# One layer of a hybrid mixer and a mixture of experts on one core: a routing step, prefetch gating and small PE products reordered

## The chip, the cores and the metric

The kernel runs on one core of one Trainium2 chip. The metric is the device time of one execution in microseconds (us). Times are medians of several runs; beside them stands one profiled execution, from which all rows below are taken. Engines are named as the profile names them: PE is TensorE, DVE is VectorE, ACT is ScalarE, POOL is GpSimd, and SP is the engine whose queue issues most of the DMAs. PEld is the loading of PE's stationary operand.

## What is computed

One layer on 1024 tokens of width 1024. A token mixer (a state-space group, a forgetting-attention group and a convolution group behind one input projection and before one output projection) is added to the input; then each token goes to one of four expert groups and, inside it, to two of eight experts. All is float32.

```python
x = x + g_m * hybrid_mixer(rms_norm(x) * (1 + sc_m) + sh_m)
h = rms_norm(x, norm_ffn_g) * (1.0 + sc_f) + sh_f
p_g = softmax(h @ w_rg + b_rg)                # 4 groups, the best one is taken
g_sel = argmax(p_g)
e_logits = (h @ w_re + b_re) of that group    # 8 experts in it
top_p, top_i = top_k(softmax(e_logits), 2)
weights = top_p / sum(top_p) * p_g[g_sel]
# for each of the 32 experts e, on the tokens that chose it:
hid = silu(xb @ w_gate[e]) * (xb @ w_up[e])   # 1024 x 512 each
y  += weight * (hid @ w_down[e])              # 512 x 1024
out = rms_norm(x + g_f * y, final_norm_g)
```

## The kernel before

**Tiling.** The 1024 tokens are eight blocks of 128 rows (`NB`), held with tokens on partitions or, transposed, with features on partitions. Every float32 product on PE is made of three: each operand is split into a rounded part and a rest (`h_hi` and `h_lo`, `xh` and `xl`, `phi` and `plo`), and hi*hi, hi*lo and lo*hi are accumulated in one bank.

**Stages.** First come the products with the conditioning vector (`ada`): chunks `at` of a weight matrix arrive by DMA, and 8 products (L415) make one piece of a row, which two products at L423 (`ps_arr`) then add up. They are spread over the input projection. `qk_tile(t)` for t = 0 to 3 (L182 to L184, `ps_pr`) makes a feature-major tile of the queries and keys, 48 products of 128x512. Between them stands the transpose of `ncu`, the negative running sum of the forget gates, into bank `ps_nc` (L487), copied to `nct` and written to HBM, from where the attention reads it back much later.

**End of the mixer.** For each row block `b` the generator `post_steps` makes the output projection (L994 to L996, `ps_wo`), adds it to the input in two halves of 512 columns (`xb`, L1000), transposes the result (`xT`), takes the root mean square, and makes the router's logits `L`: 8 products with the transposed rows as the moving operand (L1019, `ps_rt`), a copy `rT`, a transpose (L1023), and two additions into `L` (L1024, L1025). The normalized rows `h2` go to `h_d` in HBM (L1034), one DMA of 128x1024 for a block. `route_steps(b0, b1)` takes `L` of some blocks to one-hot choices `oh` and to places in the expert's list: `ps_pos` counts the tokens before a row, `ph` is the one-hot place, `Ev` the one-hot expert times the token number, and `ps_tab` = ph' x Ev is a table of token numbers by place (rows) and expert (columns). The names in the rows carry an r in front (`rohr`, `rph`, `rEv`). After the last block the table becomes the integer `toki` by four operations of DVE (L1135 to L1139): add to `tab`, find the empty places, shift by one, cast. A second use of `ph` (L1167) makes the table of weights `wtab`.

**Experts.** For expert `e` a gather by POOL (L1308, an indirect DMA with `toki`) reads its up to 128 rows of `h_d` into `xg` or `xq`; eight transposes (L1318, bank `ps_xg`) and a split give `xh`, `xl`. The weights come as 192 halves of 1 MB (two for each gate, up and down matrix) into a ring of 18 half-buffers (`NHALF`) named w, wx, wy, xq, cy; wy holds one half in two pieces. SP issues them (L1198), at most three in flight. ACT casts each half to `phi`, DVE subtracts to `plo` (L1328), and PE multiplies: 12 products of 128x512 for a half (L1340 to L1342, `ps_gu`; L1368 to L1370, `ps_d`). The same 25 products of `ident` with itself that the change uses (`WARM`, bank `ps_warm`, L292) stand at the very start of the program.

**What sets the order.** A scheduler orders the instructions of each engine from the data they need; `keep_in_program_order` (`pin` in the diff) holds an instruction at its place among the others so marked, and `tc.issue_after(ins)` or the argument of `load_half` makes an operation wait for `ins`. `NC_` + `POST` = 18 is the ring: `NC_` halves are issued before the first gather, `POST` after it. Before the change the last three of the ring wait behind three tiny memsets of POOL that follow the first gather (L1385). `row_load` and `row_spread` (L1282, `ps_row`) bring a 1024-long row of conditioning (`gf`, used at the end) to all partitions: 8 products from `sl` and two copies by ACT.

Of the kernel before, what the change touches and what calls it, by code (L numbers as in the profile page):

```python
# [12 lines left out]
F32 = mybir.dt.float32  # L13
# [9 lines left out]
P = 128  # L23
T = 1024
D = 1024
NB = 8
# [14 lines left out]
DL = 3  # L41
POST = 3
CP = 11
AN = 4
QD = 1
DC, NC_ = 2, 15
KORD = (4, 5, 6, 7, 0, 1, 2, 3)
# [27 lines left out]
def mixer_moe(ctx, tc, x, pch, prow, ada_m, ada_r, w_col, w_z, w_v, w_dtf, w_out, w_rt, w_gu, w_dn, out):  # L75
# [407 lines left out]
    for t in range(4):  # L483
        qk_tile(t)
        if t == 0:
            pc = bank("ps_nc")
            PE.transpose(pc[:32, 0:P], ncu.rearrange("p h b -> p (h b)"), ident)  # L487
            nct = sa.tile([32, P], F32, name="nct", bufs=1)
            V.tensor_copy(nct, pc[:32, 0:P])
            nc.sync.dma_start(ncum_d.rearrange("h (b k) -> (h b) k", k=P), nct)  # L490
        ada_row(*pend)
        if t == 3:
            v_split(1)
        pend = ada_acc(4 + t)
        drain(6)
# [424 lines left out]
    rank = rtp.tile([P, NB, 3], F32, name="rank")  # L920
    G.iota(vtok, pattern=[[P, NB]], base=1, channel_multiplier=1, allow_small_or_imprecise_dtypes=True)
    xsp = ctx.enter_context(tc.tile_pool(name="xsp", bufs=1, reuse_waits="tile"))
    xqs_both = xsp.tile([P, 2 * D], F32, name="xq1")
# [58 lines left out]
    def c_steps(b, yh, yl, xbs):  # L982
# [5 lines left out]
        for q in range(2):  # L988
            qs_ = slice(512 * q, 512 * (q + 1))
            ps = bank("ps_wo", "pj")  # L990
            for n, kt in enumerate(KORD):
# [7 lines left out]
                yield  # L999
            V.tensor_tensor(xb[:, qs_], ps, xb[:, qs_], op=ALU.add)  # L1000
            S.activation(ps, xb[:, qs_], AF.Square, accum_out=s2[:, q:q + 1])
# [6 lines left out]
    def post_steps(b, xb, xT, s2, h2):  # L1008
# [4 lines left out]
        if b == NB - 1:  # L1013
            tc.keep_in_program_order(V.tensor_tensor(h2, xb, ccn["af"], op=ALU.mult))
        yield
# [10 lines left out]
        yield  # L1026
        if b < NB - 1:
            V.scalar_tensor_tensor(h2, xb, s2[:, 3:4], ccn["af"], op0=ALU.mult, op1=ALU.mult)
            for q in range(2):
                hs = slice(512 * q, 512 * (q + 1))  # L1030
                (V if q else G).tensor_tensor(h2[:, hs], h2[:, hs], ccn["shf"][:, hs], op=ALU.add)
        else:
            V.scalar_tensor_tensor(h2, h2, s2[:, 3:4], ccn["shf"], op0=ALU.mult, op1=ALU.add)
        S.dma_start(h2_d[bs, :], h2)  # L1034
# [16 lines left out]
    tab = sc2.tile([P, NE], F32, name="tab", bufs=1)  # L1051
    tf = sc2.tile([P, NE], F32, name="tf", bufs=1)

    tk = []


    def route_steps(b0, b1):
# [45 lines left out]
        ohr = t_("ohr", NE, dt=F32R)  # L1103
        V.tensor_tensor(ohr, oh[0], oh[1], op=ALU.add)

# [8 lines left out]
        yield  # L1114
        phs, Evs = [], []
        for k in range(2):
            tmp = t_("el4", NE)
            V.tensor_tensor(tmp, ppv, oh[k], op=ALU.mult)
            V.tensor_reduce(pos[:, k, bl], tmp, axis=AX.X, op=ALU.add)
            ph_ = t_(f"ph{k}", P, dt=F32R)  # L1120
            V.tensor_tensor(ph_, i128[:, None, :].to_broadcast([P, n, P]), over(pos[:, k, bl], P), op=ALU.is_equal)
            Ev = t_(f"Ev{k}", NE, dt=F32R)
            V.tensor_tensor(Ev, oh[k], over(vtok[:, bl], NE), op=ALU.mult)
            phs.append(ph_)
            Evs.append(Ev)
            if not lastb:
                yield
        pq_ = bank("ps_tab")
# [3 lines left out]
        if b0 == 0:  # L1132
            V.tensor_copy(tab, pq_[:, 0:NE])
        else:
            V.tensor_tensor(tab, tab, pq_[:, 0:NE], op=ALU.add)  # L1135
        if lastb:
            V.tensor_scalar(tf, tab, 0.0, 8192.0, op0=ALU.is_equal, op1=ALU.mult)
            V.scalar_tensor_tensor(tf, tab, -1.0, tf, op0=ALU.add, op1=ALU.add)
            tk.append(V.tensor_copy(toki, tf).ins)  # L1139
        yield  # L1140
# [117 lines left out]
    run_all(post)  # L1258
    V.tensor_copy(tok_l, tf[:, NE - 1:NE])
    pc_ = bank("ps_cnt")  # L1260
# [24 lines left out]
    row_load(g_rows[0, 3072:4096], sl[0:8, :])  # L1285
    row_spread(gf, sl[0:8, :])

# [18 lines left out]
    with tc.tile_pool(name="ex", bufs=2, reuse_waits="tile") as ex:  # L1306
# [5 lines left out]
        def xpose(e):  # L1312
            xh = ex.tile([P, KT, P], F32R, tag="xh", name="xh", bufs=1)
            xl = ex.tile([P, KT, P], F32R, tag="xl", name="xl", bufs=1)
            for q in range(2):
                pt = bank("ps_xg")
                for j in range(4):
                    PE.transpose(pt[:, j * P:(j + 1) * P], xgs[e % 2][:, (4 * q + j) * P:(4 * q + j + 1) * P], ident)  # L1318
                split(xh[:, 4 * q:4 * q + 4], xl[:, 4 * q:4 * q + 4], pt.rearrange("p (j c) -> p j c", c=P))
            return xh, xl  # L1320
# [61 lines left out]
        g1 = gather(0)  # L1382
        with tc.issue_after(g1.ins):
            for h in halves[NHALF - POST:]:
                G.memset(h[0][:, 0:1], 0.0)  # L1385
        gather(1)
        for _ in range(POST):
            load_half()

# [21 lines left out]
        for e in range(NE):  # L1411
# [227 lines left out]
```

## Time and profile before

| what | value |
|---|---|
| median of 3 runs | 1276.93 us (1276.75 to 1277.41) |
| the profiled execution | 1275.77 us, of which the span from first to last instruction is 1273.9 us |
| mean granted clock of TensorE | 0.972 of full speed |
| PE busy | 1186.6 us, 93% of the span |
| DVE, ACT, POOL busy | 980.5, 736.4, 268.2 us |
| DMA | 313.21 MB, mean 246 GB/s over the span |

The page divides the span into 40 slices of 31.8 us. PE is at nine tenths or more in the slices from 650 us on, where the experts run, and the DMA engines are nearly full there; up to 620 us the mixer runs, with PE at seven to nine tenths or more. Between the two lies the routing of the last block, in which PE has little to do. All times of rows below are microseconds from the start of the span.

### The profile page before, as it was taken

The numbers are of one execution on the slowest core, as the hardware profiler recorded it, in microseconds if no ns is written. First come the engines' busy times: TensorE is split into PE (matmuls) and PEld (weight loads), VectorE is DVE, ScalarE is ACT, GpSimd is POOL, SyncE is SP. The second block draws the span as 40 slices with busy tenths as digits, with TensorE's granted clock in tenths as the row PEclk, the third lists the DMA queues.
The fourth block names the chain that finished last, engine by engine and source line by source line (L and its number), as shares of the span: only waits on it lengthen the run. The fifth ranks groups of instructions, "written<-read, shape, count | busy, mean of one in ns | idle before, by whom it ended". The sixth has DMA issues, their size and how long they took to land. (4 is left out here: it accounts for less than half of the span.)

```text
span 1273.9 us, 17238 instructions
## 1 busy us (share of the span) xinstructions
PE 1186.6 (93%) x6079; PEld 928.3 (73%) x6079; DVE 980.5 (77%) x1395; ACT 736.4 (58%) x1145; POOL 268.2 (21%) x200
## 2 busy tenths in 40 slices
PE   6999989999999779999779999999999999999993
PEld 4676757868678568778568877777877787787772
DVE  4789992145265676575559999999999999999985
ACT  4323322343354656563258877777877787777763
POOL 3110313100100353432111221122112212211112
PEclk9999999999999989999879999999999999999997
DMA  9316667633201553734889999999999999999726
GB/s 361 140 42 220 210 196 224 160 108 89 78 17 59 148 155 100 262 98 183 304 305 343 361 356 372 366 354 367 369 359 372 356 358 387 363 381 366 236 53 257
DMA packets 93339, 313.21 MB, mean 246 GB/s; under 512 B 23894, under 2 KB 34310, under 8 KB 70976
## 3 DMA queue, kind: packets, MB, share of 16 engines
q1 hardware_dynamic: 60750, 256.25, 54.8%
q10 hardware_dynamic: 14242, 32.51, 7.4%
q0 software_dynamic: 18256, 23.30, 7.2%
q8 instruction: 49, 0.80, 0.3%
q14 instruction: 42, 0.34, 0.1%
HBM read 289.22 MB, written 39.88 MB: 258 GB/s over the span
## 5 line engine op out<-in xcount | busy, mean ns | idle before, releaser
L1342 PE MATMUL ps_gu<-plo,xh 128*128 128x512 f32 x512 | 209.1, 408 | 9.1 <-DVE plo L1328 9.0
L1340 PE MATMUL ps_gu<-phi,xh 128*128 128x512 f32 x512 | 203.3, 397 | 1.4 <-ACT xh L127 1.4
L1328 DVE TENSOR_TENSOR plo<-wx,phi 128x1024 fp32r<-128x1024 f32 x166 | 198.1, 1220 | 7.8 <-ACT phi L1328 5.5
L1328 ACT CAST phi<-wx 128x1024 fp32r<-128x1024 f32 x166 | 173.1, 1054 | 50.7 <-PE ps_gu L1341 40.8
L1341 PE MATMUL ps_gu<-phi,xl 128*128 128x512 f32 x512 | 200.8, 392 | 0.0
L1378 POOL DMA_INDIRECT x_d<-early,toki x31 | 74.9, 2416 | 400.7 <-DVE early L1374 386.0
L1328 ACT CAST phi<-w 128x1024 fp32r<-128x1024 f32 x110 | 115.3, 1050 | 60.4 <-PE ps_gu L1341 53.1
L1328 DVE TENSOR_TENSOR plo<-w,phi 128x1024 fp32r<-128x1024 f32 x110 | 130.7, 1220 | 7.2 <-ACT phi L1328 6.3
L1342 PEld LDWEIGHTS ps_gu<-plo,xh 128*128 128x128 f32 x512 | 96.3, 188 | 40.2 <-DVE plo L1328 20.8
L1340 PEld LDWEIGHTS ps_gu<-phi,xh 128*128 128x128 f32 x512 | 96.5, 189 | 20.2 <-ACT xh L127 1.8
L1341 PEld LDWEIGHTS ps_gu<-phi,xl 128*128 128x128 f32 x512 | 96.5, 188 | 19.6
L1368 PE MATMUL ps_d<-phi,hh 128*128 128x512 f32 x256 | 100.4, 393 | 0.7 <-ACT hh L127 0.7
L1369 PE MATMUL ps_d<-phi,hl 128*128 128x512 f32 x256 | 100.5, 393 | 0.0
L1370 PE MATMUL ps_d<-plo,hh 128*128 128x512 f32 x256 | 96.4, 393 | 0.0
L182 PE MATMUL ps_pr<-h_hi,whi 128*128 128x512 f32 x224 | 91.5, 409 | 0.0
L184 PE MATMUL ps_pr<-h_hi,wlo 128*128 128x512 f32 x224 | 88.8, 396 | 1.3 <-POOL wlo L128 1.3
L183 PE MATMUL ps_pr<-h_lo,whi 128*128 128x512 f32 x224 | 89.2, 398 | 0.0
L225 DVE SCALAR_TENSOR_TENSOR cy<-u_t,cmw,cy 128x1024 f32<-128x1024 f32 x60 | 86.4, 1440 | 2.3 <-ACT cy L222 1.4
L128 POOL TENSOR_TENSOR wlo<-wraw,whi 128x1024 fp32r<-128x1024 f32 x14 | 40.0, 2866 | 161.1 <-ACT whi L127 142.9
L1328 DVE TENSOR_TENSOR plo<-cy,phi 128x1024 fp32r<-128x1024 f32 x44 | 53.8, 1222 | 6.0 <-ACT phi L1328 5.2
L994 PE MATMUL ps_wo<-wo_hi,yh 128*128 128x512 f32 x128 | 55.1, 431 | 2.1 <-ACT yh L127 2.1
L1368 PEld LDWEIGHTS ps_d<-phi,hh 128*128 128x128 f32 x256 | 48.3, 189 | 10.9 <-ACT hh L127 0.9
(405 smaller groups left out, 2570.9 us busy)
## 6 DMA issues: line engine op xcount, KB each, us to landing
w<-in_w_gu_dram SPq DMA_DIRECT2D x54, 1024.0 KB
wx<-in_w_gu_dram SPq DMA_DIRECT2D x50, 1024.0 KB
wx<-in_w_dn_dram SPq DMA_DIRECT2D x30, 1024.0 KB
at<-in_ada_r_dram ACTq DMA_DIRECT2D x64, 256.0 KB
cy<-in_w_gu_dram SPq DMA_DIRECT2D x11, 1024.0 KB
wy<-in_w_gu_dram SPq DMA_DIRECT2D x22, 512.0 KB
wy<-in_w_dn_dram SPq DMA_DIRECT2D x20, 512.0 KB
xq<-in_w_dn_dram SPq DMA_DIRECT2D x10, 1024.0 KB
```

The lines of the kernel that those rows point to most:

```text
L182: PE.matmul(ps, hi[:, kt, :], h_hi[hf][:, kt, :], start=(kt == 0), stop=False)
L183: PE.matmul(ps, hi[:, kt, :], h_lo[hf][:, kt, :], start=False, stop=False)
L184: PE.matmul(ps, lo[:, kt, :], h_hi[hf][:, kt, :], start=False, stop=(kt == KT - 1))
L225: yield lambda t=t, k=k: V.scalar_tensor_tensor(cy[:, :, t], v128(u_t[:, t, k:k + T]), cmw[:, t, k:k + 1], cy[:, :, t], op0=ALU.mult, op1= ...
L1328: last[:] = [S.copy(hi, raw).ins, V.tensor_tensor(lo, raw, hi.bitcast(F32), op=ALU.subtract).ins]
L1340: PE.matmul(ps, xh[:, kt], hi[:, ks], start=(kt == 0), stop=False)
L1341: PE.matmul(ps, xl[:, kt], hi[:, ks], start=False, stop=False)
L1342: PE.matmul(ps, xh[:, kt], lo[:, ks], start=False, stop=(kt == KT - 1))
L1368: PE.matmul(pd[n], hh[:, f], hi[:, ns], start=(f == 0), stop=False)
L1369: PE.matmul(pd[n], hl[:, f], hi[:, ns], start=False, stop=False)
L1370: PE.matmul(pd[n], hh[:, f], lo[:, ns], start=False, stop=(f == 3))
L1378: G.indirect_dma_start(x1_d[:, :], bass.IndirectOffsetOnAxis(ap=toki[:, e:e + 1], axis=0), yo[:, :], None, bounds_check=T - 1, oob_is_err= ...
```

## The change

It has six parts. (1) The transpose of `ncu` moves from the first `qk` tile (t = 0) to the second (t = 1), pinned. (2) In the last block (b = 7) `h2` is multiplied by `af` in halves right after each half of `xb`; the router's logits are made with the tokens on the output's partitions (`ps_rl`, 8 products of 128x36 with the rows as the stationary operand), so that `rT`, its transpose and one of the two additions go; `h2` is finished and written in two halves of 512 columns, the first before `L`, the second (`last_half[0](1)`) pinned behind the one-hot sum `ohr`. (3) In `route_steps` the table holds token number minus 1024 (`vneg`) and `tab` starts at 1024, so that empty places come out as 1024; for the last block `toki` is one operation. The two choices k = 0 and 1 go side by side through the steps behind `ps_pos`. (4) `POST` goes from 3 to 6 and `NC_` from 15 to 12: six halves wait for the first gather's landing, three more than before were held, and these three are gone from ahead of it; the three memsets go. (5) 25 products of `ident` are issued on PE behind the table's products. (6) `row_spread(gf)` moves from before the first gather into the first expert's work, behind its up product.

```diff
-POST = 3
+POST = 6
-DC, NC_ = 2, 15
+DC, NC_ = 2, 12
...
     for t in range(4):
         qk_tile(t)
-        if t == 0:
+        if t == 1:
             pc = bank("ps_nc")
-            PE.transpose(pc[:32, 0:P], ncu.rearrange("p h b -> p (h b)"), ident)
+            pin(PE.transpose(pc[:32, 0:P], ncu.rearrange("p h b -> p (h b)"), ident))
...
-            V.tensor_tensor(xb[:, qs_], ps, xb[:, qs_], op=ALU.add)
+            add = V.tensor_tensor(xb[:, qs_], ps, xb[:, qs_], op=ALU.add)
+            if b == NB - 1:
+
+                pin(add)
+                pin(V.tensor_tensor(h2[:, qs_], xb[:, qs_], ccn["af"][:, qs_], op=ALU.mult))
             S.activation(ps, xb[:, qs_], AF.Square, accum_out=s2[:, q:q + 1])
...
         if b == NB - 1:
-            tc.keep_in_program_order(V.tensor_tensor(h2, xb, ccn["af"], op=ALU.mult))
+            pr = bank("ps_rl")
+            for kt in range(KT):
+                PE.matmul(pr[:, 0:36], xT[:, kt], ccn["wrp"][:, kt, 0:36], start=(kt == 0), stop=(kt == KT - 1))
+
+            def half_h2(q):
+                hs = slice(512 * q, 512 * (q + 1))
+                pin(V.scalar_tensor_tensor(h2[:, hs], h2[:, hs], s2[:, 3:4], ccn["shf"][:, hs], op0=ALU.mult, op1=ALU.add))
+                S.dma_start(h2_d[bs, hs], h2[:, hs])
+
+            half_h2(0)
+            pin(V.scalar_tensor_tensor(L[:, b], pr[:, 0:36], s2[:, 3:4], ccn["rbias"], op0=ALU.mult, op1=ALU.add))
+            last_half.append(half_h2)
+            return
...
-        V.tensor_tensor(ohr, oh[0], oh[1], op=ALU.add)
+        so = V.tensor_tensor(ohr, oh[0], oh[1], op=ALU.add)
+        if lastb:
+            pin(so)
+            last_half[0](1)
...
         for k in range(2):
-            tmp = t_("el4", NE)
-            V.tensor_tensor(tmp, ppv, oh[k], op=ALU.mult)
-            V.tensor_reduce(pos[:, k, bl], tmp, axis=AX.X, op=ALU.add)
-            ph_ = t_(f"ph{k}", P, dt=F32R)
-            V.tensor_tensor(ph_, i128[:, None, :].to_broadcast([P, n, P]), over(pos[:, k, bl], P), op=ALU.is_equal)
-            Ev = t_(f"Ev{k}", NE, dt=F32R)
-            V.tensor_tensor(Ev, oh[k], over(vtok[:, bl], NE), op=ALU.mult)
...
+            V.tensor_tensor(Evs[k], oh[k], over(vneg[:, bl], NE), op=ALU.mult)
+        order_ = pin if lastb else lambda ins: ins
+        for k in range(2):
+            order_(V.tensor_tensor(tmps[k], ppv, oh[k], op=ALU.mult))
+        for k in range(2):
+            order_(V.tensor_reduce(pos[:, k, bl], tmps[k], axis=AX.X, op=ALU.add))
...
+        for k in range(2):
+            order_(V.tensor_tensor(phs[k], i128[:, None, :].to_broadcast([P, n, P]), over(pos[:, k, bl], P), op=ALU.is_equal))
...
         if b0 == 0:
-            V.tensor_copy(tab, pq_[:, 0:NE])
+            V.tensor_scalar(tab, pq_[:, 0:NE], float(T), None, op0=ALU.add)
+        elif not lastb:
+            V.tensor_tensor(tab, tab, pq_[:, 0:NE], op=ALU.add)
         else:
-            V.tensor_tensor(tab, tab, pq_[:, 0:NE], op=ALU.add)
-        if lastb:
-            V.tensor_scalar(tf, tab, 0.0, 8192.0, op0=ALU.is_equal, op1=ALU.mult)
-            V.scalar_tensor_tensor(tf, tab, -1.0, tf, op0=ALU.add, op1=ALU.add)
-            tk.append(V.tensor_copy(toki, tf).ins)
+
+            tk.append(pin(V.tensor_tensor(toki, pq_[:, 0:NE], tab, op=ALU.add)).ins)
...
-    row_spread(gf, sl[0:8, :])
...
-                    PE.transpose(pt[:, j * P:(j + 1) * P], xgs[e % 2][:, (4 * q + j) * P:(4 * q + j + 1) * P], ident)
+                    tp = PE.transpose(pt[:, j * P:(j + 1) * P], xgs[e % 2][:, (4 * q + j) * P:(4 * q + j + 1) * P], ident)
+                    if e == 0:
+                        pin(tp)
...
         g1 = gather(0)
-        with tc.issue_after(g1.ins):
-            for h in halves[NHALF - POST:]:
-                G.memset(h[0][:, 0:1], 0.0)
+
+        pw = bank("ps_warm")
+        for _ in range(WARM):
+            pin(PE.matmul(pw[:, 0:P], ident, ident, start=True, stop=True))
         gather(1)
         for _ in range(POST):
-            load_half()
+            load_half(g1.ins)
...
                 else:
                     next_tokens(1)
+                    row_spread(gf, sl[0:8, :])
```

**PE around the transpose of `ncu`, in the input projection.** `ps_pr` is a tile of queries and keys, `ps_arr` and `ps_a` are the conditioning row. Before:

```order
L184 MATMUL ps_pr_1408<-h_hi_106,wlo 128x512
L182 MATMUL ps_pr_1408<-h_hi_106,whi 128x512
L183 MATMUL ps_pr_1408<-h_lo_108,whi 128x512
L487 MATMUL ps_nc<-ident,ncu 32x128
L423 MATMUL ps_arr<-aacc,ind_r 128x512 x2
L415 MATMUL ps_a_1367<-at,cond_119 32x512 x8
```

and now:

```order
L183 MATMUL ps_pr_1428<-h_lo_109,whi 128x512
L184 MATMUL ps_pr_1428<-h_hi_107,wlo 128x512
L487 MATMUL ps_nc<-ident,ncu 32x128
L423 MATMUL ps_arr<-aacc,ind_r 128x512 x2
L415 MATMUL ps_a_1481<-at,cond_119 32x512 x8
L182 MATMUL ps_pr_1522<-h_hi_106,whi 128x512
```

The transpose stands one tile later: the group of L423 and L415 that was behind it now runs ahead of tile t = 1, and the 48 products of that tile stand ahead of the transpose.

**PE between the routing and the first expert.** `ps_tab` from `roh` is the table of weights, `ps_cnt` the counts, `ps_row` the spreading of a row, `ps_xg` the transposes of gathered rows. Before:

```order
L1261 MATMUL ps_cnt<-before_3980,ones_r 128x32
L1167 MATMUL ps_tab<-roh_5676,rph_5689 128x32
L1167 MATMUL ps_tab<-roh_5677,rph_5696 128x32
L1167 MATMUL ps_tab<-roh_5676,rph_5689 128x32
L1167 MATMUL ps_tab<-roh_5677,rph_5696 128x32
L1282 MATMUL ps_row<-sl,ident 128x128 x8
L1318 MATMUL ps_xg<-ident,xg 128x128 x8
L1318 MATMUL ps_xg<-ident,xq_3957 128x128 x2
L1340 MATMUL ps_gu<-phi,xh 128x512
```

and now:

```order
L1281 MATMUL ps_cnt<-before_3980,ones_r 128x32
L1407 MATMUL ps_warm<-ident 128x128
L1187 MATMUL ps_tab<-roh_5671,rph_5683 128x32
L1187 MATMUL ps_tab<-roh_5672,rph_5684 128x32
L1187 MATMUL ps_tab<-roh_5671,rph_5683 128x32
L1187 MATMUL ps_tab<-roh_5672,rph_5684 128x32
L1407 MATMUL ps_warm<-ident 128x128 x24
L1337 MATMUL ps_xg<-ident,xg 128x128 x8
L1337 MATMUL ps_xg<-ident,xq_3957 128x128 x2
L1361 MATMUL ps_gu<-phi,xh 128x512
```

The 8 row products are gone from this place, and 25 products of `ident` stand ahead of the first transpose.

**SP's queue around the first gather.** The loads of the ring, with what each waits for; DMASW4 is the landing of gather 0, Pool the memsets. Before:

```order
L1198 DMA wx<-in_w_gu_dram 128x2048 [waits DMAHW1_49]
L1198 DMA wx<-in_w_gu_dram 128x2048 [waits DMAHW6_49,DMAHW2_49,PE_49]
L1198 DMA wx<-in_w_dn_dram 128x2048 [waits DMAHW4_49]
L1276 DMA sl<-g_rows 8x128 [waits DVE_49]
L1198 DMA wy<-in_w_gu_dram 128x1024 [waits DMAHW6_49,DMASW4_49,DMASW1_49]
L1198 DMA wx<-in_w_dn_dram 128x2048 [waits Pool_49]
L1198 DMA wx<-in_w_gu_dram 128x2048 [waits DMAHW3_49,Pool_49]
```

and now:

```order
L1218 DMA wx<-in_w_gu_dram 128x2048 [waits DMAHW2_49,DMAHW0_49,PE_49]
L1296 DMA sl<-g_rows 8x128 [waits DMAHW6_49,DVE_49]
L1218 DMA wx<-in_w_gu_dram 128x2048 [waits DMASW4_49]
L1218 DMA wx<-in_w_gu_dram 128x2048 [waits PE_49]
L1218 DMA wx<-in_w_dn_dram 128x2048 [waits DMAHW1_49]
L1218 DMA wx<-in_w_dn_dram 128x2048 [waits DMAHW2_49,PE_49]
```

Three halves that stood ahead of the row's load now stand behind the gather's landing, with the three that waited for POOL.

## Rows read from the trace of the kernel before

**Rows 1.** By stages: busy time and count of each engine, granted clock, DMA share and rate.

```profile
core 0: us, PE busy (x) PEld busy (x) DVE busy (x) ACT busy (x) POOL busy (x), PEclk, DMA share, GB/s
...
175.30:178.60 3.30, 3.21 (x15) 1.14 (x19) 3.23 (x5) 0.00 (x0) 0.00 (x0) 0.50 0.81 263
623.00:629.20 6.20, 2.23 (x21) 1.39 (x21) 4.72 (x14) 1.56 (x4) 1.42 (x1) 1.00 0.96 344
629.20:641.00 11.80, 4.13 (x16) 3.71 (x16) 8.72 (x45) 3.14 (x4) 3.05 (x5) 0.50 0.93 329
641.00:653.10 12.10, 9.18 (x36) 8.14 (x37) 3.94 (x9) 2.35 (x4) 0.99 (x1) 0.50 0.96 373
700.00:800.00 100.00, 98.91 (x466) 80.50 (x465) 97.24 (x99) 77.60 (x88) 24.15 (x12) 1.00 1.00 362
```

**Rows 2.** PE's waits, 100 to 240 us: waiter, awaited, us in total, times, longest.

```profile
PE ps_nc L487 <- DVE ncu L481: 5.3, 1, 5.3
```

**Rows 3.** PE by line, 175.2 to 179 us, then 187 to 192: busy, mean ns.

```profile
L415 PE MATMUL ps_a<-at,cond 128*32 128x512 f32 x16 | 2.9, 876 | 0.0
L423 PE MATMUL ps_arr<-aacc,ind_r 128*128 128x512 f32 x2 | 1.2, 702 | 0.0
...
L415 PE MATMUL ps_a<-at,cond 128*32 128x512 f32 x16 | 1.9, 598 | 0.0
...
L423 PE MATMUL ps_arr<-aacc,ind_r 128*128 128x512 f32 x2 | 0.6, 392 | 0.0
```

**Rows 4.** In order of time, the last routing: start, us, engine, line, tiles.

```profile
626.30 1.28 DVE L1033 SCALAR_TENSOR_TENSOR h<-h,s,shf 128x1024 f32<-128x1024 f32 x1 [0.44 <-POOL s L124]
...
627.62 0.35 ACTq L1034 DMA_DIRECT2D h_d<-h  x1
...
627.79 0.26 DVE L1025 SCALAR_TENSOR_TENSOR L<-ps_rt,s,L 128x36 f32<-128x36 f32 x1
...
636.22 0.19 DVE L1135 TENSOR_TENSOR tab<-tab,ps_tab 128x32 f32<-128x32 f32 x1 [0.55 <-PE ps_tab L1131]
...
636.98 0.18 DVE L1139 CAST toki<-tf 128x32 int32<-128x32 f32 x1
637.46 1.17 POOL L1308 DMA_INDIRECT xg<-h_d,toki  x1 [11.19 <-DMA wx<-in_w_gu_dram]
...
638.97 1.71 POOL L1308 DMA_INDIRECT xq<-h_d,toki  x1 [0.16 <-issue]
```

**Rows 5.** Gathers of line L1308, 637 to 639.5 us, then all.

```profile
DMA to landing us min/median/max: 8.0/9.2/10.5
...
DMA to landing us min/median/max: 6.1/11.9/14.0
```

**Rows 6.** In order of time, PE from the places' count to the first expert.

```profile
632.65 0.39 PE L1110 MATMUL ps_pos<-rohr,tri_ltr 128*128 128x64 f32 x1 [6.29 <-DVE rEv L1123]
...
636.47 1.91 PE L1167 MATMUL ps_tab<-roh,rph 128*128 128x32 f32 x8
643.86 3.75 PE L1282 MATMUL ps_row<-sl,ident 8*128 8x128 f32 x16 [5.48 <-DMA sl<-g_rows]
647.54 1.97 PE L1318 MATMUL ps_xg<-ident,xg 128*128 128x128 f32 x8
649.57 0.66 PE L1318 MATMUL ps_xg<-ident,xq 128*128 128x128 f32 x2
...
653.41 0.40 PE L1340 MATMUL ps_gu<-phi,xh 128*128 128x512 f32 x1
```

**Rows 7.** In time, then by windows (PE, PEld, clock, DMA): L292 at the start.

```profile
9.64 8.29 PE L292 MATMUL ps_warm<-ident 128*128 128x128 f32 x50 [9.64 <-DVE ident L105]
...
14.70:18.00 3.30, 3.24 (x29) 3.05 (x27) 1.00 0.99 407
```

**Rows 8.** SP: its waits from 640 to 1250 us, then issues in time.

```profile
SPq L1198 <- DVE plo L1328: 251.0, 123, 6.0
...
624.28 3.70 SPq L1198 DMA_DIRECT2D wx<-in_w_gu_dram  x2
```

More of the change, by code (lines that the diff above doesn't have):

```diff
@@ L921, in mixer_moe @@
     G.iota(vtok, pattern=[[P, NB]], base=1, channel_multiplier=1, allow_small_or_imprecise_dtypes=True)
+    pin = lambda ins: tc.keep_in_program_order(ins)
     xsp = ctx.enter_context(tc.tile_pool(name="xsp", bufs=1, reuse_waits="tile"))
@@ L1026, in post_steps @@
         yield
[L1027 to L1033, printed above, removed]
+        V.scalar_tensor_tensor(h2, xb, s2[:, 3:4], ccn["af"], op0=ALU.mult, op1=ALU.mult)
+        for q in range(2):
+            hs = slice(512 * q, 512 * (q + 1))
+            (V if q else G).tensor_tensor(h2[:, hs], h2[:, hs], ccn["shf"][:, hs], op=ALU.add)
         S.dma_start(h2_d[bs, :], h2)
@@ L1051, in mixer_moe @@
     tab = sc2.tile([P, NE], F32, name="tab", bufs=1)
-    tf = sc2.tile([P, NE], F32, name="tf", bufs=1)
-    tk = []
+    vneg = sc2.tile([P, NB], F32, name="vneg", bufs=1)
+    G.iota(vneg, pattern=[[P, NB]], base=-T, channel_multiplier=1, allow_small_or_imprecise_dtypes=True)
+    tk, last_half = [], []
     def route_steps(b0, b1):
@@ L1114, in route_steps @@
         yield
-        phs, Evs = [], []
+        phs, Evs = [t_(f"ph{k}", P, dt=F32R) for k in range(2)], [t_(f"Ev{k}", NE, dt=F32R) for k in range(2)]
+        tmps = [t_("el4", NE), sc3.tile([P, P], F32, tag="rT", name="tm")[:, 0:n * NE].rearrange("p (b e) -> p b e", e=NE)]
         for k in range(2):
-            tmp = t_("el4", NE)
-            V.tensor_tensor(tmp, ppv, oh[k], op=ALU.mult)
-            V.tensor_reduce(pos[:, k, bl], tmp, axis=AX.X, op=ALU.add)
-            ph_ = t_(f"ph{k}", P, dt=F32R)
-            V.tensor_tensor(ph_, i128[:, None, :].to_broadcast([P, n, P]), over(pos[:, k, bl], P), op=ALU.is_equal)
-            Ev = t_(f"Ev{k}", NE, dt=F32R)
-            V.tensor_tensor(Ev, oh[k], over(vtok[:, bl], NE), op=ALU.mult)
[L1124 to L1127, printed above, removed]
+            V.tensor_tensor(Evs[k], oh[k], over(vneg[:, bl], NE), op=ALU.mult)
[4 more added lines that the diff above has]
+            order_(V.tensor_reduce(pos[:, k, bl], tmps[k], axis=AX.X, op=ALU.add))
+        if not lastb:
+            yield
+        for k in range(2):
+            order_(V.tensor_tensor(phs[k], i128[:, None, :].to_broadcast([P, n, P]), over(pos[:, k, bl], P), op=ALU.is_equal))
+        if not lastb:
+            yield
         pq_ = bank("ps_tab")
@@ L1258, in mixer_moe @@
     run_all(post)
-    V.tensor_copy(tok_l, tf[:, NE - 1:NE])
+    V.tensor_copy(tok_l, toki[:, NE - 1:NE])
     pc_ = bank("ps_cnt")
```

## The prediction

> **What bounds the kernel now.** I read the table by stages first. From 700 to 800 us, inside the experts, PE is busy 98.9 of 100 us at granted clock 1.00, and the DMA engines are full at 362 GB/s [rows 1]. There only PE's products count, and the change leaves nearly all of them as they are. So what can move the end is time in which PE stands still or runs at half clock elsewhere, and the table shows two places. One is small: at 175 us PE has waited 5.3 us for `ncu` from DVE, the only wait that the list of waits names between 100 and 240 us [rows 2], and right after it the granted clock is 0.50 for 3.3 us [rows 1]. The other is the routing of the last block. From 623 to 653 us PE is busy about half the time, and from 629.2 to 653.1 its clock is 0.50 (its lower level, 1.2 GHz) [rows 1]. There I read the order in time: the routing's DVE steps, the gather's issue at 637.46, its landing 8.0 us later, 5.5 us of PE waiting for the row that `ps_row` spreads, 3.75 us of that spreading, and the first transposes at 647.54 [rows 4 to 6]. The landing of the gather at 645.5 is already past when the transposes start: what stands ahead of them is `ps_row`, on PE itself.
>
> **Part 1, the transpose of `ncu`.** PE reached the transpose 5.3 us before DVE had made `ncu` [rows 2]. In the new order the transpose has the 48 products of tile 1 ahead of it. At full clock one takes 98.91/466 = 0.21 us [rows 1], so 48 take 10 to 11 us; PE gets there after `ncu` is made, with 5 us to spare. What goes is the wait, 5.3 us, and the half clock behind it: the same 16 passes of L415 took 2.9 us there and 1.9 at the next tile, the two of L423 1.2 and 0.6 [rows 3], so 1.0 + 0.6. Sum 6.9 us. What is late next? The group L423 and L415 now stands ahead of tile 1 and needs its `at` chunks and an ACT copy 6 us sooner; no row shows PE waiting for either in this stretch. The copy `nct` and its DMA come later, but the attention reads them only hundreds of us later. Up to 623 us PE is the busiest engine, so I take that the gain reaches 623 us. Bounds: 0, if DVE, busy 3.23 of the 3.30 us behind the wait [rows 1], holds PE a tile later, and 6.9. I take 6.9, since the waits list names no second waiter.
>
> **Part 2, the routing.** In steps.
>
> (a) `L` is ready earlier. DVE now makes half of `h2` ahead of it (half of 1.28 us) and one addition of 0.26 less [rows 4]: about 0.85. The 8 products, the copy and the transpose of the old way were beside DVE and POOL, so their going gives nothing more.
> (b) The two choices side by side spare waits between dependent steps: an estimate of 0.25, from 0 to 0.5.
> (c) `toki` took from 636.22 to 637.16 in four operations, and takes one of about 0.19 [rows 4]: 0.75.
> (d) The second half of `h2` (0.65 us of DVE) stands behind `ohr`, where DVE waits for `ps_pos` anyway.
>
> So the gather is issued about 1.9 us sooner, at 635.5. With three to six loads less in flight it lands in no more than the 8.0 us of before, by 643.5, and gather 1, 1.5 us behind it and 10.5 us on its way [rows 4, 5], by 647.5, needed some 2 us after the first transpose [rows 6].
>
> (e) `ps_row` and its wait are gone from ahead of the transposes: 647.54 is no longer set by them.
>
> (f) The 25 warm products are there instead, and they are what sets the start. 24 of them stand behind the weight table's 8 passes, which ended at 638.4 [rows 6]; 1.1 us sooner by (a) and (b), with one product in between, that is 637.6. At the program's start the same 25 products took 8.29 us, and their last 29 passes 3.24 us [rows 7]: 0.11 a pass or 0.22 a product at full clock, double that before. There it took 5.1 us of them until the passes were short. If that holds from 637.6, the clock rises at 642.7; 11.4 products are done by then, 12.6 more take 2.8 us, and the first transpose starts at 645.5 instead of 647.5.
>
> (g) From the first transpose to the first product at full speed (653.41) was 5.87 us [rows 6]. About 1.5 of it is the cast and subtraction of ACT and DVE, which don't change; the rest is PE at half clock, and halves: 1.5 + 4.4/2 = 3.7. So that product comes at 649.2, 4.2 us sooner.
>
> (h) Paid back: the 16 passes of `ps_row` now lie in the first expert. At half clock they took 3.75 us [rows 6], so 1.9 at full clock; PE's short waits for the weights' split there may hide part. DVE's six small overflow operations, two copies of ACT come with them; the nine DVE operations of 641 to 653.1, these six among them, were 3.94 us [rows 1]. Bounds 0 and 2; I take 0.8.
>
> Part 2 is 4.2 - 0.8 = 3.4 us.
>
> Bounds of (f): if the clock rises as soon as it did behind `ncu`, 3.3 us after dense work began [rows 1], the products are through by 643.2 and the gather's 643.5 sets the start: part 2 gives 5.4 to 6.2. The other end is the 9.2 us from 643.86, where `ps_row` began, to 653.1 [rows 1, 6]: by that row the clock doesn't rise within the warm products at all, and 24 of 0.45 us end at 648.4. I take the program's start, since it is the same instruction in the same number.
>
> The Trainium skill, TensorE: Matmul & The Clock Gate, Part 4 (PE-mode transpose), says that a transpose does not count as PE being busy in the way a product does. By it the stretch from 647.54, mostly transposes, should not be held against the warm products, which are plain products; this trace agrees in that the clock stayed at 0.50 through them. It makes the end at 648.4 less likely.
>
> **Part 3, the loads.** The three halves taken from ahead of the gather and the three that waited for POOL now wait for the landing of gather 0. SP's queue holds only loads and the row behind that wait, and the row is read in the first expert. Twelve halves are there when the experts start, 144 products at 0.21 us or 30 us of work; the first late half is issued at 643.5 at the latest and takes about 3 us at 362 GB/s. From 640 us on SP's waits are 251 us for DVE freeing a buffer [rows 8]: the ring stood full, so some us of DMA standing still before 643 are made up from it. I cost this at nothing; the cover is the ring's full state, and without it the price is below.
>
> **The sum.** 6.9 + 3.4 = 10.3 us. Against the profiled execution, 1275.77 us (span 1273.9 and 1.9 around it), that gives 1265.5. The profiled execution lies 1.2 us under the median of the runs, so I forecast 1266.6. 0.2% is 2.55 us, about what a measurement of this kernel can tell from no change.
>
> **Rivals.**
> A. The warm products become the new wait and don't do what they are for: the clock stays at half until they end at 648.4, and the first expert starts at half clock as before. For: 9.2 us without a rise in rows 6. Against: rows 7. Then the full-speed product comes at 648.4 + 5.87 = 654.3, 0.9 later than before, plus 0.8: part 2 costs 1.7, time 1276.9 - 6.9 + 1.7 = 1271.7.
> B. Part 1 is given back: DVE, nearly always busy there [rows 1], or a copy of ACT holds PE up to 6.9 us a tile or two later. Then only part 2 is left: 1276.9 - 3.4 = 1273.5.
> C. The late half of `h2` becomes the wait. It is issued just behind `ohr`, near 632.5, since `ps_pos` started at 632.65 [rows 6] and moves up by 0.85. The whole write before, issued at 627.62, was down by the gather's issue at 637.46, so within 9.8 us [rows 4]. As slow as that, it lands at 642.3, the gather 8.0 us later at 650.3, the full-speed product at 654.0: with 0.8 more, 1271.4. Against: fewer loads are in flight beside it, since the last half ahead of the gather is now among the two issued from 624.28 on [rows 8].
> The Trainium skill, DMA: Bandwidth & Descriptors, Anatomy of one DMA, gives each DMA a fixed cost of about 2.0 us, heaviest when it writes to HBM; by it the late half would be down near 635, just ahead of the gather, an estimate that no row here shows.
> D. Slower: the ring runs dry. If the loads of 700 to 800 us are the limit and not PE (DMA share 1.00 [rows 1]), the six halves that come late are never made up and PE pays for them: 6.3 MB at 362 GB/s are 17.4 us. It decides only from the point where SP no longer waits for freed buffers, 251 us of waiting away [rows 8]. Time 1266.6 + 17.4 = 1284.0.
>
> **How the numbers follow.** Forecast 0.62, A 0.15, B 0.13, C 0.07, D 0.03. The range takes the forecast with its bounds (down to 1276.9 - 6.9 - 6.2 = 1263.8), A and C, and leaves out B and D: 1263.5 to 1273. Faster by over 0.2% (below 1274.4): the forecast, A, C and two thirds of B, 0.92 of which I take 0.91; within 0.2%: the rest of B, and mixtures of B with A or C, 0.06; slower: D, 0.03.
>
> **What would show it.** Part 1: no wait of `ps_nc` in PE's list, clock 1.00 from 170 to 190 us, and PE's last product of the mixer, just ahead of 623 us, some 7 us sooner. (a) to (d): from there to the first gather under 13 us instead of 14.5. (f): the clock rises 7 us after the first gather's issue, during the warm products, and the first transpose follows them without a gap; a gap there says that a gather set the start. (g): under 4 us from the first transpose to full speed. (h): PE's waits in the first two experts. Part 3: no wait of PE for a cast or subtraction that itself waits for a DMA. Wrong I would be above all if PE's time to 623 us is set by DVE, or if the clock doesn't rise before the gather is there.

## The result and the profile after

The changed kernel takes 1269.52 us (median of 6 runs, 1267.92 to 1271.86) where the kernel before took 1276.84 (6 runs): ratio 0.9944, interval 0.9931 to 0.9956. That is 7.3 us faster; 10.3 were forecast (1266.6). The sign, the places and most sizes were right; one term was mis-sized by more than three microseconds, and one gain was partly given back.

To see where the time went I cut each profiled span at the same five instructions of PE: the last `ps_tr` transpose of the first phase, the first `ps_v` product, the first `ps_o` product, the start of the last `ps_wo` product (the mixer's end), and the seventh `ps_gu` product (the experts at full speed; in best_own alone the clock is still low there and rises 1.2 us later). Each row is one profiled execution, so its span can lie some us off the median of its kernel. Lengths in us:

```
                      A start   B to     C to     D mixer   E routing, F experts  span
                      to tr     ps_v     ps_o     to its    start of   to the
                                                  end       experts    end
before                 65.7    152.2     35.6     369.0      31.0      620.5     1273.9
after                  63.6    145.3     39.5     369.7      24.7      624.7     1267.3
nc_alone               65.0    145.3     35.9     368.9      31.4      621.1     1267.5
nc_back                64.0    153.3     35.6     369.2      24.6      624.6     1271.1
spread_back            66.8    145.2     36.5     369.2      29.0      620.6     1267.3
own_sl                 66.8    145.2     37.2     369.6      24.7      621.6     1265.0
v_dve                  67.8    145.2     35.8     369.3      23.8      624.4     1266.3
warm0                  66.5    145.3     35.6     369.0      20.8      623.5     1260.6
warm13                 64.5    145.2     37.2     369.4      22.2      623.0     1261.5
post3                  65.5    145.2     37.1     369.7      28.6      624.2     1270.4
spread_back_warm0      67.4    145.2     39.4     369.1      24.1      622.3     1267.4
best_spread            65.5    145.3     35.5     369.0      24.3      621.4     1261.1
best_own               64.8    145.2     35.5     369.3      23.0      620.8     1258.5
nc_v_dve               66.4    146.7     35.5     368.9      31.0      620.7     1269.3
```

The second row against the first: 2.2 us less in A, 6.9 less in B, 4.0 more in C, 0.7 more in D, 6.3 less in E, 4.2 more in F; together 6.5. On PE, ACT, DVE and POOL, A holds the same instructions in the same order in all kernels and varies from 63.6 to 67.8, so its 2.2 us are no effect of the change.

By windows, the changed kernel (columns as in [rows 1]; the windows answer those of [rows 1], the third is the stretch at the low clock):

```profile
core 0: us, PE busy (x) PEld busy (x) DVE busy (x) ACT busy (x) POOL busy (x), PEclk, DMA share, GB/s
170.00:190.00 20.00, 20.00 (x95) 14.80 (x95) 17.77 (x20) 3.77 (x6) 3.54 (x1) 1.00 0.77 248
210.90:216.50 5.60, 3.67 (x19) 3.66 (x19) 1.37 (x2) 0.96 (x2) 5.60 (x6) 0.70 0.60 166
622.60:636.30 13.70, 8.65 (x39) 8.58 (x40) 10.10 (x45) 3.25 (x4) 2.76 (x2) 0.50 0.44 160
636.30:642.70 6.40, 6.38 (x51) 5.86 (x50) 1.29 (x2) 1.16 (x3) 0.99 (x1) 1.00 0.95 365
656.80:660.20 3.40, 3.40 (x10) 2.60 (x10) 2.48 (x5) 1.58 (x3) 0.00 (x0) 0.50 1.01 415
700.00:800.00 100.00, 98.32 (x456) 79.66 (x455) 96.08 (x97) 78.12 (x89) 17.26 (x10) 1.00 1.00 360
```

The stall at 170 to 178 us is gone: PE is busy throughout, at clock 1.00. In its place there is a shorter one at 211, with the clock down behind it. The low clock of the routing lasts 13.7 us and not 24. New is a fall at 656.8 us, inside the first experts.

The stall at 211, in PE's list of waits (100 to 240 us, answering [rows 2]) and in order of time (start, us, engine, line):

```profile
PE ps_v L200 <- POOL vlo L128: 1.9, 1, 1.9
```

```profile
204.81 0.36 SPq L171 DMA_DIRECT2D wraw<-in_w_col_dram  x1
205.10 4.11 ACTq L386 DMA_DIRECT2D qk_d<-qhi  x2
...
208.76 0.45 ACTq L386 DMA_DIRECT2D qk_d<-qhi  x1
...
209.31 1.05 ACT L127 CAST vhi<-vraw 128x1024 fp32r<-128x1024 f32 x1 [4.24 <-PE ps_a L415]
...
210.43 2.35 POOL L128 TENSOR_TENSOR vlo<-vraw,vhi 128x1024 fp32r<-128x1024 f32 x1 [5.65 <-ACT vhi L127]
...
212.84 0.43 PE L200 MATMUL ps_v<-vlo,h_hi 128*128 128x256 f32 x1 [1.93 <-POOL vlo L128]
```

The row of 4.11 us holds two DMA issues of ACT's queue (ACTq). Each takes 0.45 us; the second, shown by itself below it, comes only at 208.76. In the trace it waits for the semaphore of a load that SP issued at 204.81 (`wraw`, first row), whose last update comes at 208.74. ACT's cast `vhi` stands behind it in the queue and comes late, POOL's `vlo` comes behind that, and PE, now ahead, waits 1.9 us. (The row of `vhi` names `ps_a`, the last of several semaphores by the profile; in every profile that has part 1 `vhi` starts 0.1 us behind the end of this DMA issue.)

The routing in order of time (answering [rows 4, 6]):

```profile
618.00 0.40 PE L997 MATMUL ps_wo<-wo_lo,yh 128*128 128x512 f32 x1
...
620.41 0.55 POOL L124 TENSOR_TENSOR s<-rs_ms,half 128x1 f32<-128x1 f32 x1 [10.64 <-DVE rs_ms L123]
...
621.66 0.25 DVE L1029 SCALAR_TENSOR_TENSOR L<-ps_rl,s,rbias 128x36 f32<-128x36 f32 x1
...
627.07 0.33 ACTq L1026 DMA_DIRECT2D h_d<-h  x1
...
629.57 0.19 DVE L1159 TENSOR_TENSOR toki<-ps_tab,tab 128x32 int32<-128x32 f32 x1 [0.42 <-PE ps_tab L1152]
...
631.10 1.17 POOL L1327 DMA_INDIRECT xg<-h_d,toki  x1 [10.14 <-DMA h_d<-h]
...
631.72 7.78 PE L1407 MATMUL ps_warm<-ident 128*128 128x128 f32 x48
...
639.34 1.04 PE L1337 MATMUL ps_xg<-ident,xg 128*128 128x128 f32 x8
...
642.65 0.39 PE L1361 MATMUL ps_gu<-phi,xh 128*128 128x512 f32 x1
```

and the landing of the two gathers (answering [rows 5]):

```profile
DMA to landing us min/median/max: 4.4/4.9/5.3
```

`toki` is ready at 629.8, the gather starts 1.3 us later (the row names the write of `h2`), gather 0 has landed by 635.5, and PE is still in its small products until 639.3.

### The profile page after: what moved, and what is told of

It reads as the page before. It is cut to its first block, busy times and chain, and to the rows that moved or that the text cites. A ratio compares the mean times of both kernels' runs of the same rounds, so it can differ in the third digit from the quotient of the medians.

```text
span 1267.3 us, 17336 instructions
## 1 busy us (share of the span) xinstructions
PE 1193.3 (94%) x6128; PEld 935.6 (74%) x6128; DVE 980.2 (77%) x1393; ACT 736.4 (58%) x1144; POOL 264.3 (21%) x198
## 5 line engine op out<-in xcount | busy, mean ns | idle before, releaser
L1399 POOL DMA_INDIRECT x_d<-early,toki x31 | 71.5, 2305 | 422.2 <-DVE early L1395 422.2
L1362 PEld LDWEIGHTS ps_gu<-phi,xl 128*128 128x128 f32 x512 | 96.5, 189 | 19.6
L1361 PEld LDWEIGHTS ps_gu<-phi,xh 128*128 128x128 f32 x512 | 96.7, 189 | 18.9 <-ACT xh L127 0.3
```

Source lines behind the costliest of these rows:

```text
L1361: PE.matmul(ps, xh[:, kt], hi[:, ks], start=(kt == 0), stop=False)
L1362: PE.matmul(ps, xl[:, kt], hi[:, ks], start=False, stop=False)
L1399: G.indirect_dma_start(x1_d[:, :], bass.IndirectOffsetOnAxis(ap=toki[:, e:e + 1], axis=0), yo[:, :], None, bounds_check=T - 1, oob_is_err= ...
```

## The experiments

All times are medians; before is 1276.65 to 1277.22 in each comparison, and ratios are to it, with their 95% intervals.

**nc_alone**, the kernel before with part 1 alone:

```diff
-        if t == 0:
+        if t == 1:
```

> The kernel before with part 1 alone: the transpose of ncu stands behind the second qk tile. Theory 1 (the gain is kept to the end of the mixer, as the forecast's sum has it): 6.9 us faster, about 1270. Theory 2 (given back within 60 us: PE, some 7 us ahead, waits at ps_v for POOL's vlo, which ACT starts late because its queue stands at a DMA issue, and the clock falls once more for 3.4 us behind that wait): 6.9 less about 1.9 of wait and 1.9 of half clock, so 3 us faster, about 1274, with a new wait of ps_v for vlo of 1 to 2 us in PE's list and a granted clock of 0.50 just behind it.

Measured: 1270.12 (1268.18 to 1273.41), ratio 0.9955 (0.9939 to 0.9971), so 6.9 us faster, where the interval leaves 3.7 to 7.8. Stage B is 145.3, C 35.9, and no wait of `ps_v` in its list. In this execution theory 1 held.

**nc_back**, the changed kernel with `if t == 0` again:

> The changed kernel with part 1 undone: the transpose of ncu stands behind the first qk tile again. If the parts add up, its time is the changed kernel's 1269.5 plus the 6.9 us that part 1 gave alone: 1276.4, so parts 2 to 6 together are worth 0.5 us. By the stages of the trace parts 2 to 6 win 6.3 us between the last mixer product and the experts at full speed and lose 4.2 in the experts: 1274.8. If part 1 was partly given back inside the changed kernel (wait of ps_v and the clock fall behind it), the difference to the changed kernel is smaller, 3 us: 1272.5.

Measured: 1272.97, ratio 0.9972 (0.9959 to 0.9985). So parts 2 to 6 bring 4.2 us, and part 1 only 3.5 on top of them, although it brought 6.9 alone: nearest to the third figure expected, part 1 partly given back. Stage B is 8.0 longer than in the changed kernel, stage C 4.0 shorter: C, at 35.6, has no stall.

**v_dve**, the changed kernel with the second `vlo` on DVE:

```diff
-        split(vhi[q], vlo[q], vraw[q], G)
+        split(vhi[q], vlo[q], vraw[q], V if q else G)
```

> The changed kernel with the second half of the value weights' split (vlo) subtracted by DVE and not by POOL. Theory 1 (no wait there that counts): same, 1269.5. Theory 2 (ps_v waits for vlo and the clock falls behind it): DVE takes 1.2 us where POOL takes 2.4, so the wait of 1.9 shrinks to some 0.7; if the clock then stays up, 1.2 + 1.9 = 3 us faster, about 1266.5; if it still falls, 1.2 us faster.

Measured: 1267.39, ratio 0.9918 (0.9902 to 0.9934), 2.1 us better than the changed kernel, though the two intervals just overlap. PE's waits from 100 to 252 us are now

```profile
PE ps_pr L184 <- POOL wlo L128: 1.3, 1, 1.3
PE ps_o L601 <- ACT ph L599: 0.3, 1, 0.3
```

The wait is gone, and C is 35.8. Over the eight profiles that have part 1 and `vlo` on POOL, the wait of `ps_v` and stage C go together: no wait and 35.6 or 35.9 (warm0, nc_alone), 0.7 and 36.5, 1.2 and 37.2, 1.3 and 37.1, 1.4 and 37.2, and twice 1.9 with 39.5 and 39.4. It follows how late `vhi` starts: 0.4 and 0.5 us behind the first `ps_v` product where the wait is 1.9, 1.6 and 2.2 us ahead of it where there is none. So the wait comes and goes from execution to execution, costs itself, and where it reaches 1.9 us it costs two more for the clock that falls behind it. With `vlo` on DVE C is 35.5 to 35.8 in all four profiles.

**nc_v_dve**, part 1 alone with the same edit:

> The kernel before with part 1 alone and vlo's second half on DVE. Theory 2 (part 1 loses up to 4 us in those executions in which ps_v waits for vlo, and its runs spread for that reason): a narrower spread than the 1268.2 to 1273.4 of part 1 alone, and a median at or under 1269. Theory 1 (part 1 loses nothing there): same median, 1270, and the same spread.

Measured: 1269.69 (1268.68 to 1271.06), ratio 0.9942 (0.9930 to 0.9954). The spread is 2.4 us instead of 5.2, as theory 2 has it; the median is hardly lower, and not under 1269, as theory 1 has it. In its profile stage B is 1.4 us longer than in nc_alone. These runs do not decide between the two for part 1 alone.

**spread_back**, the changed kernel without part 6:

```diff
     row_load(g_rows[0, 3072:4096], sl[0:8, :])
+    row_spread(gf, sl[0:8, :])
...
                     next_tokens(1)
-                    row_spread(gf, sl[0:8, :])
```

> The changed kernel without part 6: the row is spread ahead of the 25 small products, as in the kernel before, and the overflow operations of DVE go back with it. Theory A (the forecast's term h: the spreading costs PE 0.8 us in the first expert): PE's start of the experts comes up to 1.9 to 3.7 us later, the 0.8 are got back, so 1 to 3 us slower than the changed kernel, 1270.5 to 1272.5. Theory B (the spreading in the first expert lowers the clock for 3.4 us, and DVE, which sets the pace of the experts, gets 1.6 us of small operations more): no clock fall near 656 us, DVE's 1.6 us lie in its idle time before the experts; from the first full-speed product to the end 4 us less, of which the 16 low products ahead of the others take back up to 3: between 3 us faster and the same, 1266.5 to 1269.5.

Measured: 1268.40, ratio 0.9936 (0.9925 to 0.9948), 1.1 us better than with part 6, though the two intervals overlap. Stage E is 4.4 us longer, since the row's products now stand ahead of the 25:

```profile
631.31 3.78 PE L1302 MATMUL ps_row<-sl,ident 8*128 8x128 f32 x16
635.02 8.49 PE L1408 MATMUL ps_warm<-ident 128*128 128x128 f32 x50
643.35 1.04 PE L1338 MATMUL ps_xg<-ident,xg 128*128 128x128 f32 x8
```

and F is 4.1 us shorter, back at 620.6, with no fall of the clock near 656. That is theory B: with the move F is 4 us longer, not 0.8.

**own_sl**, the spreading late, but a tile of its own for the overflow operations:

```diff
-            V.tensor_scalar(sl, iot, vtok[:, 0:1], -1.0, op0=ALU.add, op1=ALU.add)
-            V.tensor_scalar(j7, sl[:, 1:8], float(P), None, op0=ALU.mult)
+            V.tensor_scalar(sl2, iot, vtok[:, 0:1], -1.0, op0=ALU.add, op1=ALU.add)
+            V.tensor_scalar(j7, sl2[:, 1:8], float(P), None, op0=ALU.mult)
```

> The changed kernel with a tile of its own for the overflow operations, so that DVE's six small operations no longer wait for the spreading of the row and run before the experts; the spreading stays in the first expert. Theory A (PE sets the experts' pace): same as the changed kernel, 1269.5. Theory B (DVE sets it): 1.6 us faster, 1268. If the clock still falls behind the row's products, near 656 us, the fall belongs to them and not to DVE.

Measured: 1266.63, ratio 0.9919 (0.9905 to 0.9934), 2.9 us better than the changed kernel, though the two intervals just overlap; F is 3.1 us shorter. The clock still falls, as the first window shows, so the fall does not come from DVE's operations, and the 3.1 us do not come from the fall; the second window has PE busy 99.6 of 100 us where the changed kernel has 98.3:

```profile
657.60:661.00 3.40, 3.40 (x11) 2.61 (x10) 2.16 (x3) 1.53 (x2) 0.00 (x0) 0.50 1.01 417
700.00:800.00 100.00, 99.56 (x470) 81.76 (x469) 97.59 (x100) 80.41 (x91) 21.92 (x11) 1.00 0.99 367
```

Three of DVE's operations in the changed kernel (the first and the last of the small ones, and one `plo`), and one of the same in own_sl:

```profile
657.00 0.28 DVE L1414 TENSOR_SCALAR sl<-iot,vtok 128x128 f32<-128x128 f32 x1
...
658.25 1.23 DVE L1349 TENSOR_TENSOR plo<-w,phi 128x1024 fp32r<-128x1024 f32 x1 [0.76 <-ACT phi L1349]
...
667.96 0.15 DVE L1420 CAST novi<-novf 128x1 int32<-128x1 f32 x1
```

```profile
630.78 0.28 DVE L1415 TENSOR_SCALAR sl<-iot,vtok 128x128 f32<-128x128 f32 x1
```

PE's waits for DVE's `plo`, 655 to 1225 us, changed kernel and then own_sl (us, times, longest):

```profile
PE ps_gu L1363 <- DVE plo L1349: 9.0, 27, 0.4
```

```profile
PE ps_gu L1364 <- DVE plo L1350: 7.9, 24, 0.4
```

From some expert on PE waits for DVE once in each, 0.33 us a time. The times from one expert's first `ps_gu` product to the next expert's show where that begins (us, experts 1 to 9):

```
               1     2     3     4     5     6     7     8     9
before       15.4  17.8  17.8  17.8  17.8  17.6  18.5  18.5  18.5
after        14.1  20.2  17.8  17.7  18.5  18.5  18.5  18.5  18.5
own_sl       14.2  20.1  17.8  17.8  17.8  17.8  17.8  17.6  18.5
```

An expert takes 17.8 us as long as `plo` is there in time, and 18.5, 0.7 more, from the expert on in which PE's waits for it begin: the seventh in the kernel before, the fifth in the changed one, the ninth in own_sl. So DVE works in a lead that it has at the start, and when that is used up it sets the pace. own_sl has four experts at the slower pace less than the changed kernel, 2.8 us and so nearly all of its 3.1. DVE's 1.6 us of operations thus cost more than their length, and the wait of 0.33 us is only half of the 0.7; what makes up the rest of either was not separated. Against the kernel before, the 4.2 us of F are two such experts, 1.4 us, and 2.4 us in expert 2, where PE waits for ACT's copy of `gf` and the clock is low for 3.4 us. These 2.4 stay in own_sl. That wait in the changed kernel:

```profile
PE ps_ht L1375 <- ACT gf L1303: 0.4, 1, 0.4
```

**warm0** and **warm13**, `range(WARM)` behind the gather replaced by `range(0)` and `range(13)`:

> The changed kernel without the 25 small products of part 5. Theory W (they are the new wait and buy little): the first transpose starts at the landing of gather 0, 3.8 us sooner relative to the gather's issue, but at half clock, and from it to full speed takes 5.9 us instead of 3.3; net 1.2 us faster, 1268.3. Theory N (they are needed): the clock rises only after 9 us of transposes and first products, the experts start 2 us or more later than in the changed kernel, 1271.5 or more.

> The changed kernel with 13 small products instead of 25. Theory W (the second half of them only delays the transposes, since the clock rose after 4.6 us of them and gather 0 had landed by then): they end about 6 us after they begin, the first transpose comes 2 us sooner, full speed 2 us sooner, 1267.5. Theory N: the clock does not rise before they end; the first transpose comes 2 us sooner at half clock, no gain or up to 2 us slower, 1269.5 to 1271.5.

Measured: warm0 1265.24, ratio 0.9910 (0.9895 to 0.9926); warm13 1264.71, ratio 0.9913 (0.9897 to 0.9929). Both clear the changed kernel, by 4.3 and 4.8 us. E is 20.8 and 22.2 instead of 24.7, and E and F together are 5.1 and 4.1 us shorter. warm0, PE in order of time, and the clock by windows:

```profile
632.83 1.97 PE L1337 MATMUL ps_xg<-ident,xg 128*128 128x128 f32 x8 [2.77 <-DMA xg<-h_d,toki]
...
636.67 0.40 PE L1362 MATMUL ps_gu<-phi,xl 128*128 128x512 f32 x1
```

```profile
622.90:636.50 13.60, 7.68 (x29) 6.64 (x30) 9.82 (x38) 4.42 (x6) 3.17 (x3) 0.50 0.45 158
636.50:650.00 13.50, 13.46 (x70) 10.98 (x69) 9.60 (x9) 11.45 (x14) 0.99 (x1) 1.00 1.02 414
```

Without any small product the clock is low as long here as with 25 of them in the changed kernel (13.6 and 13.7 us), and PE is in the experts' products by then. That is theory W, with a larger gain than it forecast. The stretch is not always that short: best_own, below, has no small products either and 20.5 us at the low clock.

**post3**, 15 halves ahead of the gather and three behind its landing:

```diff
-POST = 6
+POST = 3
-DC, NC_ = 2, 12
+DC, NC_ = 2, 15
```

> The changed kernel with part 4 partly undone: 15 halves are issued before the first gather and only three wait for its landing. Theory G (fewer loads beside the gathers are what let gather 0 land in 4.4 us instead of 8.0): gather 0 takes 6 to 8 us again and lands about when the small products end, gather 1 takes 8 to 10.5 and comes 2 to 4 us after the transposes could use it; full speed 2 to 3 us later, 1271.5 to 1272.5. Theory S (the small products set the start anyway): same, 1269.5.

Measured: 1271.67 (1266.20 to 1276.17), ratio 0.9959 (0.9942 to 0.9976); the median is the one that theory G put, but with this spread the interval overlaps that of the changed kernel. In the profile E is 4.0 us longer, but mostly not by the gather's flight, as theory G had it:

```profile
629.10 0.19 DVE L1159 TENSOR_TENSOR toki<-ps_tab,tab 128x32 int32<-128x32 f32 x1 [0.42 <-PE ps_tab L1152]
```

```profile
634.54 1.49 POOL L1327 DMA_INDIRECT xg<-h_d,toki  x1 [14.05 <-DMA wx<-in_w_gu_dram]
```

```profile
641.47 1.17 PE L1337 MATMUL ps_xg<-ident,xg 128*128 128x128 f32 x8 [2.61 <-DMA xg<-h_d,toki]
```

The gather starts 5.3 us after `toki`. Its row names a load; but of what it needs only the writes of `h2` can be left then, and the late half had been issued at 626.6: with loads in flight beside it that write took up to 7.9 us. Then PE idles 2.6 us behind its small products, and the clock falls once more during the transposes.

**spread_back_warm0**, **best_spread** and **best_own** put the edits together: the first is spread_back with no small products, the second adds `vlo` on DVE, the third is own_sl with no small products and `vlo` on DVE.

> The changed kernel without the 25 small products and with the row's spreading back ahead of the gather's transposes. If the spreading costs only where it stands (in the first expert: the clock and DVE's lead), and fits into PE's wait for the gather here, then from the last mixer product to full speed some 22 us and from there to the end 620.5 us: 1261 to 1262. If the row's products hold the clock low, as they did before the change, full speed comes 3 us later: 1264 to 1265.

> The same, with the second half of vlo subtracted by DVE. If the wait of ps_v and the clock fall behind it are what stood between the forecast of part 1 and its value in the changed kernel, 1 to 3 us faster than the same kernel with POOL: 1259 to 1261, and no wait of ps_v in PE's list. If not, the same.

> The changed kernel without the 25 small products, with a tile of its own for the overflow operations, and vlo's second half on DVE; the spreading stays in the first expert. If the effects add: 1269.5 less 4.3, less 2.9, less 2.1, so 1260.2. If the late spreading still costs a clock fall of 1 to 1.7 us there, it ends behind the kernel that spreads the row early.

Measured: spread_back_warm0 1265.47, ratio 0.9911 (0.9898 to 0.9924); best_spread 1264.11, ratio 0.9897 (0.9881 to 0.9914); best_own 1259.94 (4 runs, 1259.62 to 1260.34), ratio 0.9866 (0.9851 to 0.9881). The row's products were to fit into PE's wait for the gather, yet E is 24.1 and 24.3 in the two kernels that have them there, and 20.8 and 23.0 in warm0 and best_own that do not. PE in best_spread, and the stretches at the low clock in best_spread and best_own:

```profile
629.07 3.78 PE L1302 MATMUL ps_row<-sl,ident 8*128 8x128 f32 x16
...
635.02 1.94 PE L1338 MATMUL ps_xg<-ident,xg 128*128 128x128 f32 x8 [2.17 <-DMA xg<-h_d,toki]
```

```profile
621.90:639.00 17.10, 11.71 (x47) 10.70 (x48) 10.77 (x43) 5.59 (x8) 4.91 (x3) 0.50 0.52 187
```

```profile
618.50:639.00 20.50, 10.08 (x34) 8.56 (x35) 13.91 (x60) 5.47 (x7) 3.75 (x3) 0.50 0.63 231
```

The row's products of best_spread are through 2.2 us before PE has its gathered rows, so the gather sets the first transpose: 19.2 and 19.6 us after the mixer's end, against 16.5 and 18.2 in warm0 and best_own. The clock stays low 17.1 us with the row's products, 13.6 in warm0 and 20.5 in best_own without them. So what they cost in this place is not shown. best_spread has no wait of `ps_v`, as expected; its 1.4 us against spread_back_warm0 lie within the intervals. best_own, whose three edits were expected at 1260.2 together, is 16.7 us faster than the kernel before and 9.6 faster than the changed one.

## Why the prediction was right, and where it was not

**Part 1** was sized right: 6.9 forecast, 6.9 in stage B, 6.9 measured alone. The step that failed is "I take that the gain reaches 623 us". The wait that took its place is rival B's kind, a copy of ACT holding PE, on a path I had not followed: ACT's queue at a DMA that waits for a load, then `vhi`, then POOL's `vlo`. It took 4.0 us in the profiled execution, and 0 to 4.0 in others. Whether it explains all of the difference between 6.9 alone and 3.5 in the changed kernel stays open: its removal brought 2.1.

**(a) to (d)** were right in sum, 13.1 us from the mixer's last product to the gather (622.4 to 635.5 in the forecast, 618.0 to 631.1 measured), by two errors that cancel. `toki` was a microsecond earlier, since POOL's root took 0.55 us and not the 1.42 of the kernel before (why, no run shows), and then the late half of `h2` held the gather for 1.0 (it starts 1.3 us behind `toki`, 0.3 in the kernel before). So rival C's mechanism was there at a small size; post3, with more loads beside it, shows it large. The root before:

```profile
624.85 1.42 POOL L124 TENSOR_TENSOR s<-rs_ms,half 128x1 f32<-128x1 f32 x1 [11.15 <-DVE rs_ms L123]
```

**(f)** went as forecast in the clock: it rose 4.6 us into the 24 products, 5.1 were taken, and the products, not the gather, set the start. The first transpose came 21.3 us after the mixer's end, 23.1 forecast, mostly since the products begin 1.4 us sooner than forecast, with `toki`. **(g)** was 3.3 us, 3.7 forecast. What I did not ask is what would happen without the products. Rival A held that they might fail to raise the clock. They do raise it, 16.5 to 18.9 us after the mixer's end in the six profiles that have them and no row's products ahead, against 20.2 and 24.2 without (warm0 and best_own). But they stand ahead of the transposes, and that costs more: the seventh product of the experts comes at 20.8 and 23.0 us without them, at 22.2 with 13 and at 23.8 to 24.7 with 25 (28.6 in post3, where the gather is late, and 29.0 in spread_back, where the row's products stand ahead of them too). The nearest row, 9.2 us of low clock from the start of `ps_row` [rows 1, 6], misled, since it began with the row's products. In the six profiles that have these ahead of the transposes the clock rose 8.6 to 10.0 us behind their start, but 2.8 to 5.2 behind the start of the small products where those came first, and 3.7 and 6.0 behind the first transpose where nothing did (warm0 and best_own).

**(h)** is the mis-sized term: 0.8 forecast, with 2 as its upper bound, 4.2 in F. The forecast counted the spreading as PE's passes at full clock. What it left out are the fall of the clock behind them (with a short wait for ACT, 2.4 us in expert 2) and DVE's lead (two experts more at 18.5 us, 1.4). The second rested on the opening claim that only PE's products count in the experts. [rows 1] had a number against it, DVE busy 97.2 us of 100; PE's 98.9 is as high because it waits so briefly. Three of the 4.2 go when DVE's small operations lie before the experts (own_sl).

**Part 3** cost nothing, as forecast. **Rival D** did not appear: DVE waits at most some tenths for a load.

In sum: h cost 3.4 more than forecast, C up to 4.0, and E gave 2.1 more than the 4.2 forecast. So it is in part luck that the median lies only 2.9 us from the forecast: an unforeseen gain covers part of two unforeseen costs.

## What to carry to other kernels

Before costing an operation that moves into a long, nearly full stage, find which engine sets its pace: one short wait that comes back in every round names it. Work added to that engine uses up its lead, and is paid for in the rounds in which the lead is missing. Products that are there to keep PE's clock up are work too on an engine that runs in order, and an experiment without them is the first to make. A gain that puts one engine ahead lasts only if the queues that feed it are not held, as here by a DMA that waits for another one to land.

## What was not expected of the hardware

From the issue of the 128x512 write of `h2` to the start of the gather that waits for it 4.0 us passed in the changed kernel (627.07 to 631.10) and 5.6 in spread_back, with no load issued in between, and 7.9 in post3 with loads in flight; in warm0 it was 3.0, with the gather 0.3 us behind `toki` and so not held. Gathers of 128 rows landed after 4.4 to 5.3 us in the changed kernel with no loads issued until the first had landed, 8.0 to 10.5 before. The same instructions in stage A took 63.6 to 67.8 us in fourteen profiles: the two shortest, 63.6 and 64.0, have no stretch at the low clock there, the four longest, 66.8 to 67.8, have 10.2 us of it.
